# Sums of squares of the keys' and the scan output's norms: four squares, then eight matmuls in one group

## The chip, the cores and the metric

The kernel runs on one core of one Trainium2 chip. The metric is the device time of one execution in microseconds. The time before is the median of three runs; beside it there is one profiled execution, from which all lines of the profile come.

## The reference, cut to what matters

One inference step of a two-layer hybrid decoder over a prompt of 16 + 512 tokens and eight samples of 8 tokens: 592 columns of tokens in all. In each layer an FFN, a mixer and a second FFN run, with RMS norms before each. The mixer has two halves, a state-space scan and a stick-breaking attention. The change touches two norms inside the mixer:

```python
y = y.reshape(b, L, SSD_INNER) * jax.nn.silu(z.astype(f32))
yg = y.reshape(b, L, SSD_GROUPS, SSD_INNER // SSD_GROUPS)
yg = yg * lax.rsqrt(jnp.mean(yg * yg, axis=-1, keepdims=True) + EPS)
...
k = rms_norm(k.reshape(b, L, SB_HEADS, SB_HEAD_DIM), lp['k_norm'])
```

The scan output (512 channels) is normed in two groups of 256 channels, the keys (512 channels) in eight heads of 64. Each needs, for every token, sums of squares over channels. Later steps are prompt attention and attention of the samples over 2048 cached keys and values in pages, then an output projection.

## The kernel before

**Layout.** Activations lie with channels on the 128 partitions and the 592 tokens along the free dimension, so 512 channels are four tiles of 128 x 592. Dense products are written as three products of split operands (`mm3`, line 605). A sum over channels is a sum over partitions, and TensorE makes it: a matmul with a constant of ones (or of a half each, per head) as weights and the squares as the moving operand.

**The two norms.** `head_norm` (keys) and `normed` (scan output) have the same beginning. For each of the four tiles ScalarE squares it into a buffer (`hsq`, line 879; `gsq`, line 1225), and `sums` (line 469) sums it with two matmuls: the tokens' first 512 columns into PSUM bank A, the remaining 80 (64 in the second layer's scan output) into bank B. The weights have 32 columns, and tile x writes to partitions 32x to 32x+31 of the same two banks, so the four tiles use four column strips of the array. The operands are float32, for which the trace has two matmul records for each matmul. Then `by_token` (lines 484 to 491) copies the sums to SBUF on ScalarE and transposes them, `gather_sums` and `rsqrt` make the factors on VectorE, and `spread_all` spreads them over the partitions again.

**Buffers.** The squares come from the pool `tp` with six buffers under one tag "t", shared with the gates' `zi`, `zsg` and `z` tiles, the copies of the sums and others. The banks of the keys are of the pool `pg` (tag "g", three), those of the scan output of the pool `pm` (tag "pm", two).

**What sets the order.** The program is written as straight-line Python. A planner (the `TileContext`, with `schedule_with_timeline_sim=True`) orders each engine's instructions at build time, from priorities and a simulated timeline; on the chip, each engine then runs its queue in that fixed order. Priorities follow the order in which instructions are written, except where `ahead` sets another place (the tables `PRI` and `UNIT`) and where a group is made. A group is what stands inside `together`: its matmuls, written by `mm`, get a high priority from the second one on (line 211) and are chained in order; the first of them (line 208) waits for all that writes the operands of the others. The scores of the past attention (`sc`), its weighing (`po`) and the products inside the scan (`pY`, `pe`) are such groups already; the two matmuls of `sums` aren't.

**What runs around it.** In the mixer the past attention runs in steps: GpSimd gathers pages of keys and values by indirect DMA (lines 1508 and 1569) into six buffers, VectorE transposes them (`kt`, line 1519), TensorE makes the scores into the bank `sc` and weighs the values into `po`, ScalarE makes two sigmoids of each score bank (lines 1292 and 1293, `pbe` and `pst`). Between those steps the planner lays the scan, the gates, the keys' norm (`kfin` in `ORDER`), the prompt attention and the scan output's norm (`mix`).

Of the kernel before, what the change touches and what calls it, by code (L numbers as in the profile page):

```python
# [12 lines left out]
AF = mybir.ActivationFunctionType  # L13
# [93 lines left out]
class Kern:  # L107
# [354 lines left out]

        return [self.c0 + 128 * i for i in range(4)] + [self.c1 - 128]

    def sums(self, A, B, x, w, t, sel):

        n = self.c1 - self.c0 - 512
        for p, c, m in ((A, self.c0, 512), (B, self.c0 + 512, n)):
            self.nc.tensor.matmul(p[w * x:w * x + w, 0:m], sel, t[:, c:c + m], start=True, stop=True)
            yield  # L470

    def token_sums(self, out, squares, sel):

# [398 lines left out]
    def head_norm(self, T, gain, cycle):  # L872
        nc = self.nc
        A, B = self.bank("ss", None, cycle), self.bank("ss", None, cycle)
        a, b = self.c0, self.c1
        run = lambda g: [None for _ in g]
        for m, t in enumerate(T):
            s = self.tmp("hsq")
            nc.scalar.activation(s[:, a:b], t[:, a:b], AF.Square)
            run(self.sums(A, B, m, 32, s, self.c_half))  # L880
        run(self.by_token(A, B[:, 0:128], 0))
        _, r = self.rsqrt(self.gather_sums(A, B[:, 0:128], 8, 0), 8, 1.0 / 64)
        g = self.pcl(gain, self.l, 0)
        B = self.bank("hb", [128, 4, 128], cycle)
        for m in range(4):
            A = self.bank("hb", None, cycle)
            with self.together():
                run(self.spread_all(r, 2 * m, 2, A, B[:, m]))
            for p, v in self.both(A, B[:, m], T[m]):
                nc.vector.scalar_tensor_tensor(v, v, g, p, ALU.mult, ALU.mult)  # L890
# [325 lines left out]
    def normed(self, tiles, groups, gains, inv, k0):  # L1216

        nc = self.nc
        a, b, n = self.c0, self.c1, self.n
        ng = len(groups)  # L1220
        A, B = self.mis([128, 512], "gs"), self.mis([128, 128], "gs")
        run = lambda g: [None for _ in g]
        for m in range(4):
            s = self.tmp("gsq")
            nc.scalar.activation(s[:, a:b], tiles[m][:, a:b], AF.Square)
            run(self.sums(A, B, m, 32, s, self.c_ones.to_broadcast([128, 32])))
        run(self.by_token(A, B, 0))
        _, r = self.rsqrt(self.gather_sums(A, B, ng, 32), ng, inv)
        for g, grp in enumerate(groups):
            A, B = self.mis([128, 512], "gb"), self.mis([128, 128], "gb")  # L1230
            run(self.spread_all(r, g, 1, A, B))
            for m in grp:
                t = tiles[m]
                for p, v in self.both(A, B, t):
                    nc.vector.scalar_tensor_tensor(v, v, gains(m), p, ALU.mult, ALU.mult)
                self.split_f(t, k0 + m)
# [360 lines left out]
    def run(self):  # L1597
        I = self.I
        self.setup()
        for l in range(2):  # L1600
            self.ffn(I["ffn1_w_gu"][l], I["ffn1_w_down"][l], lambda m: self.norm_tile(m, "norm_mix", l),
                     None if l else self.setup_rest)
            self.norm_end()
            self.mixer(l)
            if l == 0:
                self.ffn(I["ffn2_w_gu"][l], I["ffn2_w_down"][l], lambda m: self.norm_tile(m, "norm_ffn1", 1))
                self.norm_end()
            else:
                self.ffn(I["ffn2_w_gu"][l], I["ffn2_w_down"][l], lambda m: self.store_y(m // 4) if m % 4 == 3 else None)
# [37 lines left out]
```

## Time and profile before

| | us |
|---|---|
| median of 3 runs | 2707.09 |
| lowest and highest | 2703.37, 2715.91 |
| profiled execution, own time | 2681.37 |
| its span, first to last instruction | 2679.6 |
| late part of the mixer, layer 0 | about 680 to 860 of the span |
| late part of the mixer, layer 1 | about 2000 to 2160 of the span |

In rows of the timeline the first number is the start in the span and the second the length, both in microseconds, then follow the engine (PE is the matmul, PEld the weight load, SPq the queue of loads and stores), the line, the operation, what is written and read, the shape, how many are merged in the row, and in brackets the idle time of the engine before it and what ended it. The chain of waits is followed back from the last instruction to whatever released it. In rows of stretches each engine's busy time stands with its count of instructions.

### The profile page before, as it was taken

The page shows a single profiled execution, that of the slowest core. Times are in us where ns is not written, and L with a number is a line of the kernel's source. Part 1 is how long each engine was busy: PE and PEld are TensorE (multiplying, and loading weights), DVE is VectorE, ACT ScalarE, POOL GpSimd, SP SyncE. Part 2 cuts the span into 40 slices and gives each one's busy share as a digit, 9 for nine tenths or more (in the row PEclk, how much of TensorE's full clock was granted, in tenths as well). Part 3 has the DMA queues.
Part 4 walks back from the last instruction along what each step waited for, and adds up shares of the span by engine and source line. Part 5 has one row for each costly group of instructions (what it writes and reads, how often), then busy time and mean ns, then how long its engine had stood idle before and what let it go on. Part 6 is the DMA issues. An engine that isn't in the chain of part 4 may idle for free.

```text
span 2679.6 us, 51326 instructions
## 1 busy us (share of the span) xinstructions
PE 2600.5 (97%) x21547; PEld 2466.6 (92%) x21547; DVE 1505.1 (56%) x3005; ACT 978.9 (37%) x1771; POOL 304.7 (11%) x288
## 2 busy tenths in 40 slices
PE   8999999999889999999999999999998899999999
PEld 7999999898657999999999999998886579999998
DVE  6434346397886743444554343465878957444444
ACT  3222224256564432222332222233566634223222
POOL 1000000034532100000000000001345411000000
PEclk9999999999989999999999999999998999999999
DMA  3232234467973222222222323244678731222222
GB/s 113 80 115 82 85 113 131 127 214 264 336 241 129 70 81 79 79 79 79 79 79 79 97 85 100 78 151 164 223 253 300 249 128 56 88 86 79 85 89 76
DMA packets 245112, 343.28 MB, mean 128 GB/s; under 512 B 32809, under 2 KB 196721, under 8 KB 244881
## 3 DMA queue, kind: packets, MB, share of 16 engines
q1 hardware_dynamic: 208016, 205.77, 24.7%
q0 software_dynamic: 36864, 134.23, 14.5%
q8 instruction: 169, 2.77, 0.4%
q14 instruction: 63, 0.51, 0.1%
HBM read 320.29 MB, written 19.66 MB: 127 GB/s over the span
## 4 chain that ended last, share of the span: by engine, by line
PE 84%; DVE 7%; issue 3%; ACT 3%; DMA 2%; POOL 1%; SPq 0%; DVEq 0%; POOLq 0%; ACTq 0%
PE g L605 72%; PE v L926 2%; DVE kt L1519 2%; PE po L211 1%; PE sc L211 1%; DMA v<-in_cache_v,vi 1%; DVE st L1298 1%; PE pw L476 1%; DMA kn<-in_cache_k,ki 1%; DVE pst L1298 1%; POOL v L1569 0%; PE z L208 0%; PE z L211 0%; DVE xl L447 0%; DVE wlo L596 0%
## 5 line engine op out<-in xcount | busy, mean ns | idle before, releaser
L605 PE MATMUL g<-xl,whi 128*128 128x296 f32 (+1 forms) x3392 | 1014.6, 299 | 2.7 <-DVE xl L447 2.7
L605 PE MATMUL g<-xh,wlo 128*128 128x296 f32 (+1 forms) x3392 | 1012.9, 299 | 2.0 <-DVE wlo L596 2.0
L605 PE MATMUL g<-xh,whi 128*128 128x296 f32 (+1 forms) x3392 | 1011.1, 299 | 1.5 <-DVE gs L231 1.2
L595 ACT ACTIVATE whi<-raw 128x512 fp32r<-128x512 f32 (+1 forms) x664 | 412.6, 622 | 1323.6 <-PE g L605 1240.5
L596 DVE TENSOR_TENSOR wlo<-raw,whi 128x512 fp32r<-128x512 f32 (+1 forms) x664 | 450.3, 678 | 582.8 <-ACT whi L595 529.7
L605 PEld LDWEIGHTS g<-xl,whi 128*128 128x128 f32 x3392 | 638.6, 188 | 5.6 <-DVE xl L447 3.6
L605 PEld LDWEIGHTS g<-xh,wlo 128*128 128x128 f32 x3392 | 638.7, 188 | 4.3 <-DVE wlo L596 2.5
L605 PEld LDWEIGHTS g<-xh,whi 128*128 128x128 f32 x3392 | 638.7, 188 | 4.0 <-DVE gs L231 1.4
L605 PE MATMUL g<-hl,whi 128*128 128x296 f32 (+1 forms) x1408 | 417.8, 297 | 0.0
L605 PE MATMUL g<-hh,wlo 128*128 128x296 f32 (+1 forms) x1408 | 417.6, 298 | 0.0
L605 PE MATMUL g<-hh,whi 128*128 128x296 f32 (+1 forms) x1408 | 416.7, 298 | 0.0
L1508 POOL DMA_INDIRECT kn<-in_cache_k,ki x128 | 128.3, 1003 | 1657.9 <-PE g L605 934.8
L605 PEld LDWEIGHTS g<-hl,whi 128*128 128x128 f32 x1408 | 265.2, 188 | 0.0
L605 PEld LDWEIGHTS g<-hh,wlo 128*128 128x128 f32 x1408 | 264.3, 188 | 0.0
L605 PEld LDWEIGHTS g<-hh,whi 128*128 128x128 f32 x1408 | 263.9, 188 | 0.0
L1519 DVE STREAM_TRANSPOSE kt<-kn 128x512 f32<-128x512 f32 x256 | 162.9, 681 | 27.7 <-PE sc L211 14.5
L704 DVE SCALAR_TENSOR_TENSOR x<-g,x 128x296 f32<-128x296 f32 (+1 forms) x192 | 88.1, 463 | 119.1 <-PE g L605 118.5
L1569 POOL DMA_INDIRECT v<-in_cache_v,vi x128 | 143.3, 1119 | 100.0 <-DVE kt L1519 36.1
L231 DVE TENSOR_TENSOR us<-g,R 128x296 f32<-128x296 f32 (+1 forms) x176 | 81.5, 464 | 129.1 <-PE g L605 129.0
L231 DVE TENSOR_TENSOR gs<-g,R 128x296 f32<-128x296 f32 (+1 forms) x176 | 80.6, 463 | 126.2 <-PE g L605 121.3
L691 ACT ACTIVATE hh<-us 128x592 fp32r<-128x592 f32 (+1 forms) x88 | 61.2, 696 | 64.3 <-DVE us L689 64.3
L605 PE MATMUL g<-mh,whi 128*128 128x296 f32 (+1 forms) x256 | 77.7, 312 | 2.4 <-ACT mh L1277 1.3
(372 smaller groups left out, 2838.8 us busy)
## 6 DMA issues: line engine op xcount, KB each, us to landing
raw<-in_ffn_w_gu SPq DMA_DIRECT2D x176, 512.0 KB
raw<-in_ffn_w_down SPq DMA_DIRECT2D x80, 512.0 KB
raw<-in_w_in SPq DMA_DIRECT2D x44, 512.0 KB
raw<-in_w_out SPq DMA_DIRECT2D x16, 512.0 KB
spill<-x SPq DMA_DIRECT2D x16, 296.0 KB
x<-spill SPq DMA_DIRECT2D x16, 296.0 KB
raw<-in_ffn_w_down SPq DMA_DIRECT2D x16, 256.0 KB
xt<-in_x_prompt SPq DMA_DIRECT2D x8, 256.0 KB
```

The lines of the kernel that those rows point to most:

```text
L211: i = self.nc.tensor.matmul(*a, **k).ins
L231: self.nc.vector.tensor_tensor(tv[0:P, h, :], ps[h][0:P, 0:self.n], rv[0:P, h, :], ALU.mult)
L595: nc.scalar.activation(hi[:, 0:nk], s, AF.Copy)
L596: nc.vector.tensor_tensor(lo[:, 0:nk], s, hi[:, 0:nk].bitcast(F32), ALU.subtract)
L605: mm = nc.tensor.matmul(ps[h][:, 0:self.n], w[:, k, :], self.hv(x)[:, h, :], start=(first and k == 0 and i == 0), stop=(last and k == nk - ...
L691: nc.scalar.activation(hh[:, a:b], u[:, a:b], AF.Copy)
L704: nc.vector.scalar_tensor_tensor(v, p, 0.5, v, ALU.mult, ALU.add)
L926: nc.tensor.matmul(ps[c], x[:, t0:t0 + 128], w.rearrange("p x c -> p (x c)"), start=(k == 0 and i == 0), stop=(k == 7 and i == 2))
L1298: self.nc.vector.tensor_tensor_scan(sv, sv, self.zero[0:rows].to_broadcast([rows, b - a - 1]), 1.0, ALU.mult, ALU.add)
L1508: self.nc.gpsimd.indirect_dma_start(kn, None, self.kflat, bass.IndirectOffsetOnAxis(ap=self.kidx[self.l][:, s, 2 * i + u:2 * i + u + 1], a ...
L1519: self.nc.vector.transpose(kt[:, 2 * u:2 * u + 2].rearrange("p t h i -> p t (h i)"), kns[u][:, :, 256 * quad:256 * quad + 256])
L1569: self.nc.gpsimd.indirect_dma_start(v.rearrange("p k c -> p (k c)"), None, self.vflat, bass.IndirectOffsetOnAxis(ap=self.vidx[self.l][:, s ...
```

## The change

The method `sums` goes, and `side_sums` takes its place. Both norms now make all four squares first and then call it once. It writes the same eight matmuls inside `together` with `mm`, the bank A of all four tiles first, then bank B of all four. Shapes, operands and results are the same.

```diff
-    def sums(self, A, B, x, w, t, sel):
+    def side_sums(self, A, B, squares, sel):
 
         n = self.c1 - self.c0 - 512
-        for p, c, m in ((A, self.c0, 512), (B, self.c0 + 512, n)):
-            self.nc.tensor.matmul(p[w * x:w * x + w, 0:m], sel, t[:, c:c + m], start=True, stop=True)
-            yield
+        with self.together():
+            for p, c, m in ((A, self.c0, 512), (B, self.c0 + 512, n)):
+                for x, t in enumerate(squares):
+                    self.mm(p[32 * x:32 * x + 32, 0:m], sel, t[:, c:c + m], start=True, stop=True, skip_group_check=True)
...
+        sq = []
         for m, t in enumerate(T):
-            s = self.tmp("hsq")
-            nc.scalar.activation(s[:, a:b], t[:, a:b], AF.Square)
-            run(self.sums(A, B, m, 32, s, self.c_half))
+            sq.append(self.tmp("hsq"))
+            nc.scalar.activation(sq[m][:, a:b], t[:, a:b], AF.Square)
+        self.side_sums(A, B, sq, self.c_half)
...
+        sq = []
         for m in range(4):
-            s = self.tmp("gsq")
-            nc.scalar.activation(s[:, a:b], tiles[m][:, a:b], AF.Square)
-            run(self.sums(A, B, m, 32, s, self.c_ones.to_broadcast([128, 32])))
+            sq.append(self.tmp("gsq"))
+            nc.scalar.activation(sq[m][:, a:b], tiles[m][:, a:b], AF.Square)
+        self.side_sums(A, B, sq, self.c_ones.to_broadcast([128, 32]))
```

## The prediction

> **What bounds the kernel now.** I read the page first, its busy shares and the chain that ended last, then the busy time of stretches, then the chain in the stretches where the change lies.
>
> ```profile
> PE 2600.5 (97%) x21547; PEld 2466.6 (92%) x21547; DVE 1505.1 (56%) x3005; ACT 978.9 (37%) x1771; POOL 304.7 (11%) x288
> PE 84%; DVE 7%; issue 3%; ACT 3%; DMA 2%; POOL 1%; SPq 0%; DVEq 0%; POOLq 0%; ACTq 0%
> ```
>
> TensorE holds 84% of the chain, but that is an average over the dense products of the two FFNs and the mixers. The squares and their sums lie inside the mixers, where the past attention, the scan and the prompt attention run beside each other. There the stretches of 20 us (span; busy time of PE, PEld, DVE, ACT and POOL; granted clock; DMA share; GB/s) look otherwise:
>
> ```profile
> 680.00:700.00 20.00, 17.62 (x212) 13.53 (x210) 16.08 (x33) 12.71 (x25) 10.15 (x10) 1.00 1.01 367
> 780.00:800.00 20.00, 17.36 (x156) 10.63 (x153) 17.95 (x44) 13.79 (x28) 5.20 (x6) 1.00 0.88 314
> 2020.00:2040.00 20.00, 17.05 (x226) 12.82 (x222) 16.56 (x45) 11.56 (x29) 8.23 (x8) 0.83 0.90 332
> 2120.00:2140.00 20.00, 16.29 (x167) 10.70 (x160) 18.39 (x51) 13.00 (x26) 8.26 (x7) 1.00 0.69 251
> ```
>
> In the four stretches of the change PE stands idle 2.4 to 3.7 us in 20, VectorE is as busy as it is, and the DMA share is 0.69 to 1.01. So a microsecond of PE saved here isn't a microsecond of the kernel. The chain of waits over these stretches, layer 0's keys, layer 0's scan output, then layer 1 (start, length, what; left-out pieces between), says who holds the end:
>
> ```profile
> 693.54 8.62 DMA kn<-in_cache_k,ki
> ...
> 787.75 2.03 DVE xc L1263 x3
> ...
> 792.88 1.13 DVE st L1298
> ...
> 2018.55 2.69 PE ss L469 x11
> 2021.43 0.70 PE sc L211 x27
> ...
> 2124.22 0.69 ACT gsq L1225
> 2124.95 1.73 PE gs L469 x5
> 2126.70 0.60 ACT sums L484
> ```
>
> Layer 0's keys lie wholly under a gather of 8.62 us, layer 0's scan output under VectorE. Only layer 1 has the sums on the chain, 2.69 and 1.73 us.
>
> **The change part by part.** It removes and adds no instruction: 16 squares and 32 matmuls (64 records, two to a matmul). It moves the sums of one place together and makes the first of them wait for the last square.
>
> *What the sums take now.* The busy time of line 469 alone in its four stretches (span, PE, PEld):
>
> ```profile
> 694.80:697.20 2.40, 2.28 (x16) 0.99 (x16) 1.00 1.02 401
> 787.80:794.40 6.60, 4.73 (x16) 1.43 (x16) 1.00 1.06 402
> 2018.40:2021.40 3.00, 2.90 (x16) 1.40 (x16) 1.00 1.03 391
> 2122.50:2126.80 4.30, 3.22 (x16) 1.43 (x16) 1.00 1.08 382
> sum 16.30, PE 13.13 PEld 5.24; mean PE 3.28 PEld 1.31
> ```
>
> *What a group takes.* Grouped matmuls onto other column tiles stand in the trace, and so does one square's pair of sums alone:
>
> ```profile
> 700.93 0.94 PE L211 MATMUL sc<-kt,qbd 128*32 128x128 f32 x27
> 701.68 1.05 PE L211 MATMUL po<-v,wt 128*32 128x256 f32 x16
> 793.19 1.18 PE L469 MATMUL gs<-gsq,call 128*32 128x512 f32 x4
> ```
>
> One pair alone is four records, 2 x 512 + 2 x 80 = 1184 columns in 1.18 us, 1.0 ns a column. The group of `po` has 16 records of 256, 4096 columns in 1.05 us, 0.26 ns a column: four tiles at a time. A group of the sums has 16 records and 4736 columns, so 4736 x 0.26 = 1.2 us, no longer than one pair now. Four groups take 4.8 us, and 13.1 - 4.8 = 8.3 us of PE time come free.
>
> [...]
>
> *How much reaches the end.* The copy of the sums must wait for the last square and one pair behind it. That is so before and after. Line 469's own view says who waits for it and what it waits for, and the timeline shows the first and the last square of the scan output and the copy in layer 0, and its four squares in layer 1:
>
> ```profile
>   issue: 5.4, 20
>   ACT gsq L1225: 3.1, 4
>   ACT hsq L879: 0.2, 1
> who waited for it (us, times):
>   ACT sums L484: 1.9, 2
> ...
> 786.57 0.70 ACT L1225 ACTIVATE gsq<-xc 128x592 f32<-128x592 f32 x1 [1.03 <-DVE xc L1263]
> ...
> 792.28 0.70 ACT L1225 ACTIVATE gsq<-xc 128x592 f32<-128x592 f32 x1
> 794.27 0.60 ACT L484 ACTIVATE sums<-gs 128x512 f32<-128x512 f32 x1 [0.74 <-PE gs L469]
> ...
> 2121.44 1.35 ACT L1225 ACTIVATE gsq<-xc 128x576 f32<-128x576 f32 x2
> ...
> 2124.21 1.35 ACT L1225 ACTIVATE gsq<-xc 128x576 f32<-128x576 f32 x2 [1.43 <-DMA x<-spill]
> ```
>
> Everything that ever waited visibly for these matmuls is 1.9 us, in two waits. The last square ends at 792.98, its pair runs 793.19 to 794.37 and would be replaced by a group of the same 1.2 us that starts at the same instant. So those 1.9 us stay. In layer 1 the last pair of squares starts at 2124.21 and ends 1.35 us later, again with one pair behind it: the same.
>
> For the keys the copies don't wait. In layer 0 they lie under the gather above. In layer 1 the next scores are late, and this is the one place where a gain could come:
>
> ```profile
> 2017.69 2.44 ACT L879 ACTIVATE hsq<-k 128x592 f32<-128x592 f32 x4
> 2020.52 0.46 ACT L1293 ACTIVATE pst<-sc,bq 128x256 f32<-128x256 f32 x1
> 2021.03 0.11 PEld L208 LDWEIGHTS sc<-kt,qbd 128*32 128x32 f32 x1 [0.27 <-ACT pst L1293]
> 2022.95 0.94 POOL L1508 DMA_INDIRECT kn<-in_cache_k,ki  x1 [8.18 <-PE po L211]
> ```
>
> The scores start at 2021.03, the moment that ScalarE has read the score bank (2020.52 + 0.46), and ScalarE came to that behind the four squares (2017.69 + 2.44 = 2020.13) and a copy. The 2.69 us of sums on the chain therefore lie beside squares and a sigmoid that end no earlier. The group would start at 2020.13 and end near 2021.3: the scores slip 0.2 to 0.3 us if they stand behind it, nothing if ahead.
>
> *Waits and buffers added.* Behind the waiting group on PE stands whatever the planner put there: scores, weighing, transposes; gathers wait for those, as POOL's 8.18 us show. Four square tiles are alive at once out of six buffers. The loads of z in SP's queue share these buffers and may get theirs only behind the group:
>
> ```profile
> 696.15 5.40 SPq L1262 DMA_DIRECT2D z<-zd  x4
> 785.81 0.73 DVE L1263 TENSOR_TENSOR xc<-xc,z 128x592 f32<-128x592 f32 x1
> ```
>
> They are first read 84 us after the last is issued (785.81 - 701.55), so a delay of some 2 us costs nothing. The two PSUM banks are taken at the first matmul and so held shorter, by up to the 5.7 us between the first square's end and the last's; no wait for `gs` above the 1.9 us speaks of anybody who would profit.
>
> *The sum.* Gain, bounds: nothing to 8.3 us. I take 1 us, near nothing, because of the four places only one (2.69 us) both lies on the chain and is free of a wait just behind it. Loss, bounds: nothing to 16.9 us (below). I take 0.3 us, the slip of the scores. Net -0.7 us: the profiled execution's span of 2679.6 and its own time of 2681.4 would become 2678.9 and 2680.7. The median of the runs, 2707.1, is 1% above the profiled time, so the same difference is taken off the median: **2706.4 us, no change**.
>
> **The rivals.** The order on each engine is planned at build from priorities and simulated times, so eight matmuls that go to one place can shift what stands around them until the mixer ends. The unit of such shifts is one step of the past attention; two successive groups of scores in layer 0:
>
> ```profile
> 708.52 0.30 PE L208 MATMUL sc<-kt,qbd 128*32 128x128 f32 x1
> 715.76 0.30 PE L208 MATMUL sc<-kt,qbd 128*32 128x128 f32 x1
> ```
>
> *Faster: a step is won in each layer.* With 8.3 us of PE free the plan can put scores ahead of the sums, and the gathers, which wait for them, start sooner. A step is 7.24 us, twice is 14.5 us: 2692. For it: the 8.18 us that POOL waited in layer 1. Against it: in layer 0 neither place has PE on the chain, and VectorE is the fuller engine later on.
>
> *Slower: PE stands before the group.* The first matmul holds PE's queue until the fourth square is done. If the plan thinks the squares nearer to each other than ScalarE runs them, scores and weighing behind the group wait. Between the end of the first square and that of the last lie 787.27 to 792.98 = 5.7 us in layer 0's scan output (1.2 us and more of other work runs between two squares), 1.8 us at each of the keys (three more squares of 0.6 us) and 2122.1 to 2125.6 = 3.5 us in layer 1's scan output: 12.8 us. With a group of 1.0 us before the scores each time, 16.9 us: 2724. It decides from about 13.5 us on, that is, when nearly all of these stalls reach the gathers. For it: PE does wait on these squares now (3.1 us in four). Against it: the plan can fill PE ahead of the group with the work that it now puts between and behind the pairs.
>
> *The change doesn't do what it says: the tiles run one after another.* Then a group takes 4 x 1.18 = 4.7 us and the copy comes 3.5 us later at the three places with no gather above them: 10.5 us, 2717. Against it: the `sc` and `po` rows, with the same kind of weights (128 x 32) into one bank.
>
> **How the numbers follow.** Chances: no change 0.57, with a range of its own of 2694 to 2719 (gain and loss up to half a percent, which is about what a measurement of this kernel can tell from nothing); tiles one after another 0.03, also within that; a step won 0.22; PE stands 0.18. So faster by over 0.5% 0.22, within 0.60, slower 0.18. The range runs past the two rivals' times, 2692 and 2724, by 4 to 6 us, about the spread of the runs shown on one side of their median: 2686 to 2728, which leaves out about a tenth at each end.
>
> **What would show it.** Right: line 469's busy time near 4.8 us instead of 13.1, each group about 1.2 us long, the copies of the scan output's sums still 1.1 to 1.3 us behind the last square, the idle time of PE in the late mixer larger by about 7 us, and the end of both mixers within a few microseconds of now. Wrong toward faster: PE's idle time there unchanged and the gathers' wait for scores shorter. Wrong toward slower: an idle PE of several us just before the first matmul of a group, ended by a square, with scores behind it. Groups of 4 us would show that the tiles don't run together.

## The result: slower by 0.9%, and the loss that the traces show is in layer 0's mixer

| | before | after |
|---|---|---|
| median of the runs, us | 2707.38 (4 runs, 2703.37 to 2715.91) | 2735.02 (4 runs, 2731.26 to 2738.51) |
| ratio, 95% interval | | 1.0092 [1.0064, 1.0120] |
| profiled execution, own time and span | 2681.37, 2679.6 | 2731.26, 2729.5 |

A repeat of both kernels in a later round (e17 below) gave 1.0065 [1.0044, 1.0086]. Ratios compare fast runs alone; one of the eight runs of e1 (2879.26 us, at a granted clock of 0.834) is slow and isn't in its ratio. The forecast was 2706.4 with a range up to 2728: the kernel is slower and lies outside the range.

The page of the kernel after, engines and the chain that ended last:

```profile
PE 2626.8 (96%) x21547; PEld 2478.3 (91%) x21547; DVE 1505.6 (55%) x3005; ACT 978.4 (36%) x1771; POOL 305.1 (11%) x288
PE 87%; DVE 5%; ACT 4%; issue 2%; DMA 1%; another core or an unknown queue 0%; SPq 0%; POOL 0%; DVEq 0%; ACTq 0%; POOLq 0%
```

The counts are the same as before, to the instruction. Busy PE has grown by 26 us against the first profile of before, but that isn't the change: two later profiles of before (e4 and e15) have 2626.6 and 2622.7 us. The page can't say where the time went.

One caution first. The first profile of before is of a quick execution: the median is 26 us above it, and the two later profiles of the same program have spans of 2712.9 and 2711.4. So "span after minus span before" (50 us) isn't the effect. What can be compared is stages. Here is layer 0 behind the keys, cut at six events read off each timeline: the first square of the scan output, the first matmul that spreads the norm's result (`gb`), the end of the past attention's last weighing (`po`), the end of the prompt attention's last weighing (`zo`), the first matmul of the prompt's tail (`z` from `qt`), and the last addition of the mixer. Stretch; length; busy time of PE, PEld, DVE, ACT and POOL; granted clock of PE; DMA share; GB/s. First the kernel before, from its first profile:

```profile
786.57:807.61 21.04, 17.69 (x149) 10.92 (x145) 17.36 (x48) 14.95 (x30) 3.35 (x4) 0.92 0.55 203
807.61:837.47 29.86, 24.33 (x292) 17.05 (x290) 26.22 (x59) 19.08 (x38) 13.36 (x12) 0.94 0.62 212
837.47:842.18 4.71, 4.29 (x49) 3.59 (x50) 3.33 (x10) 1.04 (x3) 0.00 (x0) 1.00 0.00 0
842.18:845.66 3.48, 3.48 (x42) 2.97 (x41) 1.19 (x9) 3.18 (x7) 0.00 (x0) 1.00 0.41 153
845.66:920.18 74.52, 72.69 (x583) 70.35 (x583) 51.26 (x93) 30.81 (x55) 10.13 (x6) 0.98 0.19 60
```

Then the kernel after:

```profile
796.22:822.68 26.46, 20.20 (x208) 12.60 (x204) 18.65 (x50) 14.86 (x30) 6.81 (x7) 0.81 0.46 153
822.68:848.56 25.88, 20.84 (x200) 13.34 (x200) 15.11 (x34) 9.84 (x19) 8.26 (x8) 0.80 0.61 217
848.56:862.87 14.31, 9.77 (x77) 6.78 (x76) 11.35 (x27) 10.28 (x21) 0.00 (x0) 0.75 0.01 1
862.87:878.44 15.57, 15.57 (x99) 13.71 (x99) 4.62 (x19) 5.44 (x10) 0.00 (x0) 0.68 0.23 79
878.44:952.72 74.28, 70.33 (x563) 67.78 (x563) 51.48 (x90) 29.85 (x52) 10.40 (x6) 0.98 0.19 57
```

Read it line by line. From the first square to the first spread it costs 5.4 us more, and the next stage gives 4.0 us back: the past attention ends 1.4 us later. Then comes the loss. From the past's end to the prompt's end it takes 14.31 us instead of 4.71 (+9.6), and from there to the tail 15.57 instead of 3.48 (+12.1). The last stage is as long as it was. Together +22.9 us (156.50 against 133.61). The later profile e15 of before, whose execution was not a quick one, has 20.81, 30.89, 4.94, 4.82 and 74.52 for the same stages; against it the loss is 20.5 us, 20.1 of them in the third and fourth. Counted from the mixer's first query square it is 17.5 us (485.4 against 467.9), and the two spans differ by 18.1 (2729.5 against 2711.4).

The fourth stage isn't idle time: PE has no gap in it, and 41 of its 99 matmul records (6.9 us) are of the output projection, which in before come behind the tail's `z`. Over all five stages PE is idle 19.8 us, in e15 12.3.

Layer 1's mixer is 482.7 us long in after (first query square to last addition), and 461.4, 482.6 and 475.4 in the three profiles of before: a single trace can't tell whether layer 1 has changed.

The rows of PE that stand for the two lost stages (start, length, engine, line, operation, what is written and read, shape, count, and the idle time before it with what ended it), kernel after:

```profile
847.75 0.82 PE L211 MATMUL po<-v,wt 128*32 128x256 f32 x11
...
849.86 0.59 PE L211 MATMUL z<-k,q 64*128 64x384 f32 x1
...
853.00 0.22 PE L1326 MATMUL z<-mall 128*128 128x128 bf16 x1 [1.40 <-ACT st L1343]
853.14 0.48 PE L208 MATMUL z<-k,q 64*128 64x256 f32 x1
...
854.82 0.66 PE L1353 MATMUL zt<-call,be 128*128 128x128 f32 x4 [0.97 <-ACT st L1343]
...
862.02 0.85 PE L211 MATMUL zo<-wp,vk 128*64 128x128 f32 x5
...
864.70 1.97 PE L1443 MATMUL ptn<-call,tb 64*128 64x64 f32 x8
...
874.58 0.27 PE L208 MATMUL pon<-wp,vk 64*64 64x64 f32 x1
...
878.44 0.41 PE L208 MATMUL z<-k,qt 64*32 64x264 f32 x1
```

And the kernel before in its third profile (e15):

```profile
838.23 0.59 PE L211 MATMUL z<-k,q 64*128 64x384 f32 x1
...
841.52 0.48 PE L208 MATMUL z<-k,q 64*128 64x256 f32 x1
...
849.91 0.82 PE L211 MATMUL po<-v,wt 128*32 128x256 f32 x11
...
853.32 1.10 PE L1440 MATMUL ptn<-call,tb 64*128 64x64 f32 x8
...
854.97 0.72 PE L211 MATMUL zo<-wp,vk 128*64 128x128 f32 x5
...
858.36 0.32 PE L208 MATMUL pon<-wp,vk 64*64 64x64 f32 x1
...
860.50 0.41 PE L208 MATMUL z<-k,qt 64*32 64x264 f32 x1
```

The prompt attention comes in twelve units per layer, each a chain over engines: `z` on PE, sigmoids on ScalarE, a product on VectorE, transposes `zt`, a copy, and `zo` on PE. In before, the `z` of the last two units (64x384 and 64x256) stand on PE ahead of the past's last weighing, so their sigmoids run beside it. In after both stand behind it. When the past is done, two whole chains are left, and nothing else is there to fill PE: it waits for sigmoids (1.40 and 0.97 us in the rows), and its granted clock falls to 0.75. Behind them comes the new tokens' own attention (`ptn`, `pwn`, `pon`), whose `ptn` lay ahead of the last `zo` before, and then the tail, whose `z` takes the two banks of the pool `pm` over from it: 10 us from `ptn` to `pon` where it was 5, with matmuls of the output projection between.

### The profile page after: what moved, and what is told of

The parts are those of the page before. It is cut to its first block, busy times and chain, and to the rows that moved or that the text cites. A ratio compares the mean times of both kernels' runs of the same rounds, so it can differ in the third digit from the quotient of the medians.

```text
span 2729.5 us, 51318 instructions
## 1 busy us (share of the span) xinstructions
PE 2626.8 (96%) x21547; PEld 2478.3 (91%) x21547; DVE 1505.6 (55%) x3005; ACT 978.4 (36%) x1771; POOL 305.1 (11%) x288
## 4 chain that ended last, share of the span: by engine, by line
PE 87%; DVE 5%; ACT 4%; issue 2%; DMA 1%; another core or an unknown queue 0%; SPq 0%; POOL 0%; DVEq 0%; ACTq 0%; POOLq 0%
PE g L606 73%; PE v L928 2%; PE po L211 2%; PE sc L211 1%; DVE kt L1522 1%; PE z L208 1%; PE pw L477 1%; PE sc L208 1%; DVE st L1301 1%; DMA v<-in_cache_v,vi 1%; PE po L208 0%; ACT st L1343 0%; PE z L211 0%; DMA kn<-in_cache_k,ki 0%; ACT be L1342 0%
## 5 line engine op out<-in xcount | busy, mean ns | idle before, releaser
L1522 DVE STREAM_TRANSPOSE kt<-kn 128x512 f32<-128x512 f32 x256 | 162.7, 680 | 29.1 <-PE sc L211 12.3
L211 PE MATMUL po<-v,wt 128*32 128x256 f32 x1000 | 84.9, 421 | 4.3 <-issue 3.9
```

Of the source, the lines that this page charges most:

```text
L211: i = self.nc.tensor.matmul(*a, **k).ins
L1522: self.nc.vector.transpose(kt[:, 2 * u:2 * u + 2].rearrange("p t h i -> p t (h i)"), kns[u][:, :, 256 * quad:256 * quad + 256])
```

## The experiments

An order edge (`add_manual_dep` with a dependency of the kind NoSync, shortened in the diffs) makes one instruction stand behind another in the plan and adds no work. Letters in the quoted expectations name theories: **B**, PE stands idle before the keys' group; **D**, the plan of the work around the scan output's group has changed; **E**, the group itself costs time. D', F and G are later forms of D. Ratios are to the kernel before on the same chip, with 95% intervals. The length of a mixer is read off the timeline, from its first query square to its last addition.

### First round: which norm, which part

**e1, the group in the scan output's norm alone** (keys as before).

```diff
 # head_norm of the kernel after
-        self.side_sums(A, B, sq, self.c_half)
+            run(self.sums(A, B, m, 32, s, self.c_half))
```

> The scan output's norm with the group, the keys' norm as before. Theory A (the loss comes behind the scan output's group, where the plan of all engines changes from there to the end of the mixer): 12 to 30 us slower than before, 0.5 to 1.1%. Theory B (PE stands before the keys' group for the fourth square): within 5 us of before. Theory C (any edit that moves the plan costs something of this size, wherever it lies): slower too, so this run alone does not tell A from C.

1.0091 [1.0059, 1.0123]: the whole loss. **e2, the group in the keys' norm alone:**

> The keys' norm with the group, the scan output's norm as before. Theory A: within 8 us of before. Theory B: 12 to 30 us slower. Theory C: slower by some amount, with a plan that changes behind the keys' group.

1.0017 [0.9997, 1.0037]: nothing, or a trace. So PE's wait for the keys' squares in the kernel after, here that of layer 0 (1.27 us in e2's own trace), is paid by nobody, and B falls:

```profile
702.31 0.62 PE L208 MATMUL ss<-hsq,call 128*32 128x512 f32 x1 [1.28 <-ACT hsq L881]
```

**e3, all four squares first but the sums ungrouped, in both norms:**

```diff
-        self.side_sums(A, B, sq, self.c_half)
+        for m in range(4):
+            run(self.sums(A, B, m, 32, sq[m], self.c_half))
```

> All four squares are written first in both norms, the eight matmuls behind them not grouped (each pair waits for its own square). Theory A and B (it is the group that costs): within 5 us of before. If writing the squares first is what costs (buffers held, the plan moved): 12 to 30 us slower.

0.9998 [0.9974, 1.0022]. The order of the squares alone does nothing. **e4, the kernel before again:**

> The kernel before once more, for a second profile of it. Its first profiled execution lay 26 us under the median of its runs; if the difference is the time at half the granted clock, this one shows a longer span and more of it.

0.9995 [0.9969, 1.0020], span 2712.9 us at a mean granted clock of 0.981, where the first profile has 2679.6 at 0.987: longer, and with less clock, as expected.

### Second round: the group, or the order around it

**e5, the kernel after with the four matmuls of bank B ahead of those of bank A.** The same eight matmuls, the same wait for four squares, in one group.

```diff
-            for p, c, m in ((A, self.c0, 512), (B, self.c0 + 512, n)):
+            for p, c, m in ((B, self.c0 + 512, n), (A, self.c0, 512)):
```

> The changed kernel with its two loops' banks exchanged: in each group the four short matmuls into bank B first, then the four long ones. The same matmuls, the same wait, the same group. In the plan of layer 0 the last scores of the past attention then stand behind the first spread of the factors and the prompt attention is as far along as before, which isn't so in the changed kernel. Theory D (what costs is the order that the plan takes behind the group in layer 0, with the prompt attention's last blocks put back): within 8 us of before. Theory E (the group costs by itself, by its wait or its width): 20 to 30 us slower, as the changed kernel.

1.0010 [0.9994, 1.0026]: **the loss is gone.** A group that does the same work in another order of its members costs nothing that these runs can measure; E falls. What differs is the planned order behind it: the last two units' `z` are ahead of the past's last weighing again.

**e6, the group without the raised priority of its matmuls.**

> The changed kernel, but the eight matmuls of a group keep the priority of their place; the chain and the common wait stay. The plan has the same order around the group as the changed kernel. Theory D: 20 to 30 us slower than before, as the changed kernel. If the high priority is what costs: within 8 us of before.

1.0066 [1.0041, 1.0091], two runs. The order on PE at the places read (the spread, new keys, last units, tail) is that of after, and so is the loss: the raised priority isn't it.

**e7, after, with the past's last scores held behind the first spread in layer 0 by an order edge; e8, before, with the first spread held behind the last scores.** This was the first difference seen between the orders: in before the last group of scores stands behind the first `gb`, in after ahead of it.

```diff
+            # e7
+            self.tc.add_manual_dep(self.first_sc, self.sp[0].name, NoSync)
+            # e8
+            self.tc.add_manual_dep(self.sp[0], self.last_sc.name, NoSync)
```

> The changed kernel with one order added in layer 0: the last scores of the past attention come behind the first spread of the scan output's factors, as in the plan of before. Theory D: at least half of the loss comes back, 0 to 12 us slower than before. Theory E: 20 to 30 us slower.

> The kernel before (no group) with one order added in layer 0: the first spread of the scan output's factors comes behind the last scores of the past attention, as in the plan of the changed kernel. The prompt attention stays as far along as before. Theory D in its narrow form (those two places exchanged are the cause): 12 to 28 us slower than before. If it is the prompt attention's place that matters: within 6 us. Theory E: within 5 us.

e7: 1.0016 [1.0003, 1.0029]. e8: 1.0087 [1.0070, 1.0104]. Taken by ratios, this looks like a proof. By the traces it isn't: in e8 layer 0, where the edge is, is 461.0 us long, shorter than in e4 (466.3), while layer 1, where no edge is, is 481.6; in e5, e6 and e7, the other profiles of that round, layer 1 has 465.2, 461.8 and 456.2. The planner had laid layer 1 anew, and it was the slow one. An edge moves more than it names, so a ratio alone proves nothing here.

### Third round: the new keys' place, a theory that fell

In after, the new tokens' attention (`zn` ...) starts on PE ahead of one more block of the prompt's transposes (60 of 80 ahead of it instead of 68). D' took this for the cause.

```diff
+        # e9, kernel before, layer 0
+        self.tc.add_manual_dep(self.blk[9][0], zn[0].name, NoSync)
+        # e10, kernel after, layer 0 (e11: blk[11])
+        self.tc.add_manual_dep(zn[0], self.blk[9][-1].name, NoSync)
```

> The kernel before, no group, with one order edge in layer 0: the transposes of the prompt attention's unit 9 stand behind the first matmul of the new keys on PE, as they do in the kernel after (60 of the 80 transposes ahead of the new keys instead of 68). Theory D' (the plan is what costs: new keys ahead of the prompt's last blocks): layer 0's mixer ends later by 10 to 17 us than in the second profile of before (466.3 us from its first query square), the last zo by 5 to 9 us (386.7 there), and the kernel is slower, 2.72 ms where before is 2.707 (ratio 1.004 to 1.009). Rival, the past attention's weighing or the spread's place does it and new keys' place costs nothing: ratio within 0.999 to 1.002, layer 0's mixer end 462 to 468 us. Layer 1's plan has also moved (new keys behind 152 transposes instead of 148, as in after): by the rows of after that is worth -2 to +1 us.

> The kernel after, with the group in both norms and one order edge in layer 0: the new keys' first matmul stands behind the transposes of the prompt attention's unit 9 (68 ahead of it, as in before). Theory D': layer 0's mixer end comes back from 485 us to 464 to 470, the kernel to a ratio of 0.998 to 1.003 against before. Rival, another part of the moved order does it: ratio stays at 1.006 to 1.010 and layer 0's mixer end at 480 us or over.

> The kernel after, with one order edge in layer 0: the new keys stand behind all 80 transposes of the prompt attention. Theory D': prompt attention ends at or before 387 us in layer 0 (395 in after); what the new keys lose by it is the tail's start, since the tail's pair of banks waits for them; net, the mixer ends at 455 to 475 us, ratio 0.995 to 1.004. Rival: stays at 1.006 to 1.010, with the mixer's end at 480 us or over.

> The kernel before, no group, with an order edge in both layers: the new keys stand behind all 80 transposes of each layer's prompt attention (68 in layer 0 and 148 of 160 by layer 1 in before). Theory D', that a prompt block sooner is worth about 8 us at its end: both mixers end by 0 to 12 us sooner, ratio 0.992 to 1.000. Rival, the tail's banks wait for the new keys and the mixer ends later by what they are put back: ratio 1.001 to 1.008.

| | ratio | layer 0's mixer, us |
|---|---|---|
| e9 | 1.0024 [1.0007, 1.0040] | 466.5 |
| e10 | 1.0029 [1.0009, 1.0049] | 488.2 |
| e11 | 1.0079 [1.0060, 1.0098] | 481.1 |
| e12 | 1.0028 [1.0010, 1.0046] | 471.5 |

D' missed on nearly everything; of its forecasts only the ratio of e10 came. With the new keys early (e9) layer 0 is as before, and the ratio lies between the two forecasts; with the keys back in their place (e10) layer 0's one trace is as long as in after. e12, which puts them behind the whole prompt attention in both layers, loses 0.28%, some 7 us over two layers: late new keys alone are no explanation for the 18 to 28 us of after.

With these traces there was something better than one difference between two orders: a mark that sorts every layer. In layer 0 the `z` of the prompt's last unit stands ahead of the past's last weighing in before, e2 to e5, e7 to e9 and e12, and behind it in after, e1, e6, e10 and e11; in layer 1, behind it only in e8 and e11. e10 apart, which lost only 0.3%, the kernels that have it behind somewhere are those that lost most.

### Fourth round: one unit

**e13, before, the last unit's `z` behind the last weighing in layer 0; e14, after, the last weighing behind that `z`; e15, before, for its trace.**

```diff
+        # e13, kernel before, layer 0; far[0] is the unit's first matmul
+        self.tc.add_manual_dep(self.far[0], self.last_po.name, NoSync)
+        # e14, kernel after, layer 0
+        self.tc.add_manual_dep(self.weigh0, self.z_mm.name, NoSync)
```

> The kernel before, no group, with one order edge in layer 0: the first matmul (z) of the prompt attention's last unit stands on PE behind the past's last weighing (64 po matmuls), as it does in the kernel after. Up to that place the order is that of before. Theory F (this one exchange is the loss: the unit's chain z, sigmoids, transposes, zo begins only when the past is done, and the new keys' values and the tail come behind it): the last zo ends 8 to 15 us behind the last po instead of 4.7, the tail begins 15 us or more later, layer 0's mixer ends 12 to 20 us later (466 us before on such a chip, 478 to 486 here), ratio 1.004 to 1.010, with no group in the kernel at all. Rival (the exchange only goes along with the loss, which comes from the 4 to 7 us by which the prompt is late already at the group): layer 0 within 5 us of before, ratio 0.999 to 1.003.

> The kernel after, with the group in both norms, and one order edge in layer 0: the past's last weighing stands behind the z matmuls of the prompt attention's last unit, as it does in before. Up to that place the order is that of after (the last scores ahead of the first spread, 60 transposes ahead of the new keys). Theory F: the last zo ends 4 to 6 us behind the last po, layer 0's mixer ends at 464 to 470 us, ratio 0.997 to 1.003. Rival: layer 0 at 478 us or over, ratio 1.006 to 1.010. Layer 1's plan moves as well, without a forecast for it.

> The kernel before as it is, for its trace on the same chip: the unit's z ahead of the last weighing in both layers, layer 0's mixer 454 to 467 us long, ratio 0.998 to 1.002 by every theory.

e13: 1.0030 [1.0011, 1.0049]. e14: 1.0010 [0.9993, 1.0026]. e15: 1.0003 [0.9982, 1.0024]. By its ratio the undoing (e14) took the loss away nearly whole, with the group still in both norms. Its one trace doesn't agree with F: the prompt outlasts the past by 9.1 us (forecast 4 to 6), and layer 0's mixer is 479.1 us long (forecast 464 to 470), in an execution 7 us above the median of e14's runs. The doing (e13) brought only a third to a half of the loss, a ratio that F had ruled out and its rival had not: F was too narrow. (The profiled run of e13 had a mean granted clock of 0.937, all its other runs 0.978 to 0.986, and it is 12 us above its median; its trace is used for the order only.) The trace said why: one unit behind leaves 8.3 us of prompt attention when the past is done. In after it is 14.3, with two units behind.

### Fifth round: two units

**e16, before, no group, the last two units' `z` behind the last weighing in layer 0; e17, after again on the same chip.**

```diff
+        # e16, kernel before, layer 0
+        self.tc.add_manual_dep(self.far[10], self.last_po.name, NoSync)
```

> The kernel before, no group, with one order edge in layer 0: the z matmuls of the prompt attention's last two units (10 and 11) stand on PE behind the past's last weighing. From that place on the order of layer 0 is that of the kernel after nearly instruction for instruction; up to it, that of before. Theory G (the cost is the prompt attention left over when the past attention is done: its chain then runs alone, PE stands idle in it and is granted half its clock): the last zo ends 13 to 15 us behind the last po (14.3 in after, 8.3 with one unit behind, 4.7 in before), layer 0's mixer ends at 482 to 492 us, its part at half clock is 30 us or more behind the spread (before 10, after 40), the kernel is slower by 15 to 27 us, ratio 1.0055 to 1.010. Rival H (the loss is in what stands ahead of that place, the scan output's group and the past's scores ahead of the spread): ratio 1.001 to 1.004, like e13.

> The kernel after as it is, for its trace and its granted clock beside those of before on one chip: ratio 1.006 to 1.012 by either theory; theory G adds that about two thirds of the loss is a lower mean granted clock (0.975 to 0.979 where before has 0.982 to 0.984) and the rest, time at full clock, is 3 to 8 us.

e16: **1.0054 [1.0034, 1.0074]**. e17: **1.0065 [1.0044, 1.0086]**. One order edge in the kernel before, without any group, brings five sixths of what the change brings on the same chip. The ratio is just under G's range, which began at 1.0055, and above H's, which ended at 1.004; the intervals of e16 and e17 overlap, so the missing sixth isn't shown to be there. The two lost stages in e16, where the columns are those of the stage tables above:

```profile
847.02:860.31 13.29, 9.16 (x60) 6.22 (x60) 11.06 (x26) 10.28 (x21) 0.00 (x0) 0.67 0.01 1
860.31:875.32 15.01, 15.01 (x100) 13.17 (x100) 4.62 (x19) 5.44 (x10) 0.00 (x0) 0.72 0.24 82
```

They are those of the kernel after (14.31 and 15.57 us, clock 0.75 and 0.68), with PE busy 9.16 us in the first and without a gap in the second. Layer 0's mixer is 484.0 us long, 467.9 in e15, and layer 1's, whose plan has moved too, 472.7 against 475.4: the loss is in layer 0. H (the loss lies ahead of that place) falls: the order of PE in e16 is that of e15 until the `z` of unit 10, and behind it nearly that of after.

The time by which the prompt attention outlasts the past attention (end of the last `zo` less end of the last `po`), beside the ratio:

| kernel | layer 0, us | layer 1, us | ratio |
|---|---|---|---|
| before (e4; e15) | 4.7; 4.9 | 0.6; 0.6 | 0.9995; 1.0003 |
| e3, e2 | 5.0, 4.8 | 0.6, 5.0 | 0.9998, 1.0017 |
| e5, e9 | 5.9, 6.2 | 4.7, 5.7 | 1.0010, 1.0024 |
| e12 | 4.1 | 4.1 | 1.0028 |
| e7, e14 | 8.4, 9.1 | 6.4, 4.3 | 1.0016, 1.0010 |
| e10, e13 | 8.2, 8.3 | 6.9, 7.5 | 1.0029, 1.0030 |
| e11 | 9.3 | 9.2 | 1.0079 |
| e16 | 13.3 | 4.7 | 1.0054 |
| after (first; e17), e1, e6 | 14.3 in all four | 3.5; 3.5, 2.1, 3.5 | 1.0092; 1.0065, 1.0091, 1.0066 |
| e8 | 2.9 | 15.7 | 1.0087 |

Every kernel with 13 us or more in one layer is slower by 0.5% or more; every kernel with 9.1 or less in both stays within 0.3%; e11 has over 9 in both. Added over the two layers the numbers sort e11 too: the kernels with 16.4 us or more (after, e1, e6, e8, e11, e16) lose 0.5% or more, those with 15.9 or less at most 0.3%. It is a mark and not a price, since 15.9 and 16.4 lie close together and their losses don't. The time from the last `zo` to the tail is no such mark: e12 has 15.3 and 15.1 us there in its two layers, as long as after in layer 0, and loses 0.28%. No kernel of the study is measurably faster than before.

## Why the prediction was wrong

**The group: right, at full clock.** The keys' group in layer 0 takes what was forecast (span, busy PE, clock, DMA share, GB/s):

```profile
702.00:704.00 2.00, 1.20 (x16) 1.00 0.88 328
```

16 records and 4736 columns in 1.20 us, where one pair alone, a quarter of the columns, took 1.18: the four column tiles run at once, and the rival "one after another" is out. The scan output's groups fell into half clock:

```profile
802.90:805.30 2.40, 2.20 (x16) 0.50 0.90 362
2184.00:2187.00 3.00, 2.15 (x16) 0.53 1.05 409
```

With the keys' group of layer 1 at 1.2 us again, that is 6.75 us instead of 13.13, not 4.8. Four tiles at a time and the size of 1.2 us were right; that a group may run at half clock, as the two rows of 2.20 and 2.15 us do, was left out.

**The copies of the sums: off by the same.** Forecast 1.1 to 1.3 us behind the last square. In layer 0 the last square ends at 801.93 + 0.70 = 802.63, the copy starts 2.8 us later:

```profile
801.93 0.70 ACT L1228 ACTIVATE gsq<-xc 128x592 f32<-128x592 f32 x1
802.99 1.06 PE L208 MATMUL gs<-gsq,call 128*32 128x512 f32 x1
805.45 0.59 ACT L485 ACTIVATE sums<-gs 128x512 f32<-128x512 f32 x1
```

Some 1 us of that is the half clock, by an estimate: the group takes 2.20 us where the keys' takes 1.20. By itself this would have stayed within the forecast: e5 has the same group in layer 0, 2.20 us at a clock of 0.50, and costs nothing measurable.

**The keys: right as far as measured.** "The copies don't wait", "the scores slip 0.2 to 0.3 us": e2 agrees by its time; the slip itself wasn't read off a row. PE's idle time before the keys' groups, the sign named as "wrong toward slower", is there (the 1.28 us shown with e2) and means nothing.

**"The end of both mixers within a few microseconds of now": wrong for layer 0,** by some 20 us. One sign of being right came all the same, by luck: PE's idle time "larger by about 7 us" is there in layer 0 (19.8 us in the five stages, 12.3 in e15), but 4.1 us of the difference are waits in the third stage, which the prediction didn't have, and not PE time come free.

**The step that failed** is the term of the loss, "Loss, bounds: nothing to 16.9 us", and the sentence under the rivals that sized a shift: "The unit of such shifts is one step of the past attention", 7.24 us. The prediction saw that eight matmuls that go to one place can shift what stands around them until the mixer ends, and that is just what happened. But it priced the shift by the past attention, which was the busy, visible flow at the place of the change, and took the slower rival as stalls of PE in front of the groups. The runs show another thing in its place: the past attention ends hardly later, while the prompt attention beside it falls two units behind and is left over at its end, and moving those two units by one order edge (e16) costs 0.54% without any group. A first estimate of that price could have been read in the profile of before. The stages from the past's end to the tail were 8.2 us there because the prompt's last chains lay under the past's last weighing; without that cover they are 30 us. The upper end of 2728 fell short of 2735 for this.

**How much is the clock.** Every run has a mean granted clock of PE. On e17's chip it is 0.9823 in before (mean of 21 runs) and 0.9787 in after (10 runs). Time x (1 - clock) grows from 48.0 to 58.1 us, about 10 of the 18 us between the mean times (G had forecast two thirds). In e16 it is 6 of 15. That is an estimate from the mean clocks, and an upper bound for what the clock costs, since part of the half clock falls on time in which PE waits (in a stretch below, 2.0 of 7.23 us): of the 16.5 us between the spans of e17 and e15, 9.2 are idle time of PE and 7.3 busy time (2630.0 against 2622.7 us).

The last part of layer 0's mixer in after, cut where the clock changes and where PE's gaps end (the columns of the stage tables):

```profile
847.75:855.64 7.89, 5.35 (x58) 3.29 (x50) 4.20 (x9) 4.62 (x11) 0.00 (x0) 1.00 0.00 0
855.64:862.87 7.23, 5.23 (x33) 3.79 (x34) 7.15 (x19) 5.66 (x12) 0.00 (x0) 0.50 0.01 2
862.87:871.05 8.18, 8.18 (x40) 6.73 (x41) 1.81 (x7) 3.73 (x7) 0.00 (x0) 0.50 0.30 112
872.71:878.44 5.73, 5.73 (x54) 5.32 (x53) 2.81 (x12) 1.02 (x2) 0.00 (x0) 1.00 0.12 27
```

The clock halves after a stretch in which PE was busy 5.35 of 7.89 us and never waited longer than the 1.40 us of the row shown above. It then stays halved through 8.18 us in which PE has no gap, all of it transposes and products with the identity (`tm`, `ptn`, `pwn`), and is full again at 872.71, 1.66 us after the first product of the output projection. What sets it to half and back isn't shown. Over the whole execution the clock not granted is 1.8% in before and 2.1% in after, by the means of 0.9823 and 0.9787; in e16, which differs from before only in the order of the work, it is 2.0% (0.9801).

**What stays open.** Why the planner lays the prompt's last units behind the past in one case and not in the other wasn't followed into its simulated timeline; that it does so with the banks in one order and not in the other (e5) shows how near the two plans lie. e10 and e14 have a long layer 0 in their one trace (488.2 and 479.1 us) and a small loss in their ten and twelve runs; the ratio decides, the profiled executions are 7 us above the medians, and why those traces are long is open. e12 and e9 lose 0.2 to 0.3% with the prompt in time, through late new keys and an altered layer 1 perhaps; that is argued, not shown.

## What to carry to other kernels

When a planner orders the engines, a small edit has two prices: what its instructions cost, and what the new plan costs. Test the second by a null edit (the same instructions in another order of the group): if that removes the loss, the work of the edit isn't what costs, and the plan around it is. To price a new plan beforehand, look at where two flows end side by side, and ask what each costs when the other is no longer there to cover it; here that stretch, and not the place of the edit, held the loss. And check an order edge by the trace of every stage, since it also moves stages that it doesn't name.

## What the runs showed of the hardware

The same program differs from round to round as much as by the costliest edit here: medians of before are 2710.85, 2686.63, 2713.61, 2714.22 and 2711.68 us in the five rounds. In the second, before's mean clock x time is 2645 us, in the others 2663 to 2665, so the difference of some 24 us is mostly not the granted clock. Nor is it shown to be the chip: the first two rounds are on record with the same chip number. The first profile of before (2681.37 us at 0.987, a product of 2646) is of the quick kind; only ratios taken in one round hold. And PE at half clock shows as a group of the same 16 records that takes 2.20 us where the keys' takes 1.20, 1.8 times as long; its first row of 512 columns is 1.06 us where the keys' is 0.62.
